# Loading the attention stages' weights and modulation tiles from GpSimd's queue instead of SyncE's

## The chip, the cores and the metric

The kernel runs on one core of a Trainium2 chip. A core has five engines, each with its own queue of instructions that it works off in order: TensorE (PE in the profile, with its weight loads shown apart as PEld), VectorE (DVE), ScalarE (ACT), GpSimd (POOL) and SyncE (SP). SP does no arithmetic; here it issues DMA transfers. Any of these queues can hold a DMA issue, and an issue that has to wait (for its target buffer to come free, say) holds up what stands behind it in the same queue. The transfers themselves run on 16 DMA engines that all queues share.

The metric is the time in microseconds (us) of one execution on the chip; less is better. Times of kernels are medians of several executions.

## The reference

A decoder trunk of two layers, for one sequence of 512 positions and 1024 features, in float32. A conditioning vector `c` gives, for each layer, six vectors of modulation (shift, scale and gate for each half of a layer). Cut to what matters here:

```
for layer in range(2):
    mod = silu(c) @ w_mod[layer] + b_mod[layer]        # 1024 x 6144, split into six vectors
    shift1, scale1, gate1, shift2, scale2, gate2 = split(mod, 6)
    h = rmsnorm(x, g_attn[layer]) * (1 + scale1) + shift1
    proj = h @ w_in[layer]                             # q, k, v of three groups of heads, and fz
    qa, ka, qb, kb = rotary(qa, ka, qb, kb)
    oa = differential_attention(qa, ka, va, lam)       # 4 heads (A)
    ob = dilated_mixture_attention(qb, kb, vb)         # 6 heads (B)
    oc = forgetting_attention(qc, kc, vc, cumsum(log_sigmoid(fz + bias)))   # 6 heads (C)
    x = x + gate1 * (concat(oa, ob, oc) @ w_out[layer])
    h = rmsnorm(x, g_mlp[layer]) * (1 + scale2) + shift2
    u, g = split(h @ w_up[layer])
    x = x + gate2 * ((silu(causal_conv3(g)) * u) @ w_down[layer])
return rmsnorm(x, g_final)
```

## The kernel before

**Layout and precision.** The activations are kept feature-major: `x` is a tile of 128 partitions, 8 chunks of features and 512 positions. Each operand of a big product is split into a high and a low part of float32r, and a product is three matmuls (`mm3`, L250 to L253): high by high, high by low, low by high. The weights are split on the chip: a raw weight tile of 128 x 1024 (512 KB) is loaded (`raww`), ACT copies its high part (L174, `whi`), and DVE subtracts to get its low part (L186, `wlo`).

**The weight pipeline.** `plan` lists all weight tiles of the program in the order of use. The class `Weights` walks along it: `dma` issues loads (L148) into a pool of 3 raw buffers, `hi` and `lo` make the two parts (a pool of 2 pairs), and `use` hands them to the matmuls. `pump`, called once per chunk of a product, keeps loads two tiles ahead and splits one tile ahead. A load waits until `wlo` of the tile three places earlier has been made, since that frees its buffer.

**The modulation.** `mod_stream` (L211 on) loads a row block of `w_mod` of 512 KB (L214, `rawm`) into a pool of 2 buffers, and DVE multiplies and sums it into a column of `modc` (L217). In the startup the first 16 blocks come in as `mu` (L1010) and are multiplied on POOL (L1036, then summed on ACT, L1037) or reduced on DVE; blocks 16 to 39 of layer 0 are streamed during layer 0's attention, the remaining 56 during layer 0's MLP.

**The attention of a layer** (`layer_attn`) works through eight pairs of heads in the order B0 B1 A0 C0 A1 C1 B2 C2. For each pair, 8 blocks of 128 queries go through scores, mask and maximum (DVE, L641), exponential (ACT), transposition, splitting and the product with the values; the loop runs over 64 blocks, with the second half of a block two blocks behind. Between these pieces `fill` puts the next pair's projections (`qkps`, L251 to L253) and values, and at the end the first parts of the output projection. `tick` advances small generators: `qk_post` copies a projection out of PSUM (`qf`, L456) and, for kinds A and B, needs its even and odd partitions exchanged for the rotation, which two DMA copies of 128 KB do (`sw`, L458 and L459); for kind A another 24 small copies stack the split rows (L477), for kind C `stack_gen` splits the rows (L420 on DVE, L434 on ACT) and copies in bias rows from `aT` (L443). `fz_post` runs the chain for the forget gate: a polynomial on DVE (`z`, up to L529), a cumulative sum on PE (`pf`, L537), its scaling on DVE (L541), the filling of a tile `au` with ones on POOL (L550) and the copying of values into it (L552, L553).

**What sets the order.** The Python code gives the order in which instructions are recorded; a scheduler of the framework then sets the order in each engine's queue by its own estimates, with some instructions told to come after others (`issue_after`). In the version before, all of the loads and copies named above are issued by SP (`nc.sync`), so `raww`, `rawm`, `sw`, `qk` and the bias rows stand in one queue; POOL has two small loads (`bm`, `gA`), the eight multiplications of `mu`, and the two fills of `au`.

Of the kernel before, what the change touches and what calls it, by code (L numbers as in the profile page):

```python
# [30 lines left out]
def kernel(  # L31
# [25 lines left out]
    nc = tc.nc  # L57
    PS = bass.MemoryType.PSUM
    V, A, T, G = nc.vector, nc.scalar, nc.tensor, nc.gpsimd
# [25 lines left out]
    def tick():  # L85
        for g in list(aux):
            if next(g, StopIteration) is StopIteration:
                aux.remove(g)
# [27 lines left out]
    for l in range(DEPTH):  # L116
# [16 lines left out]
        for m in range(KC):  # L133
            for b in range(0, FC, 8):
                n = min(8, FC - b)
                plan += [(wdown[l, m, :, 128 * b:128 * (b + n)], 128 * n, "wp" if m < 7 else "hs")]

    class Weights:
        def __init__(self):
            self.raw, self.w = {}, {}  # L140
            self.nd = self.nh = self.nl = self.nu = 0
            self.pt = None

        def dma(self, upto):
            while self.nd < min(upto, len(plan)):
                src, n, at = plan[self.nd]
                t = rawp.tile([128, 4 * VZ], F32, tag="raw", name="raww")
                nc.sync.dma_start(out=t[:, 0:n], in_=src)  # L148
                self.raw[self.nd] = t
                self.nd += 1  # L150

# [57 lines left out]
    W = Weights()  # L209

    def mod_stream(l, ci):  # L211
        part, m = divmod(ci, 8)
        raw = mrp.tile([128, 1024], F32, tag="raw", name="rawm")
        nc.sync.dma_start(out=raw, in_=wmod[l, ci])  # L214
        yield
        dst = modc[:, l, ci:ci + 1]
        V.tensor_tensor_reduce(out=raw, in0=raw, in1=scb, scale=1.0, scalar=bm[:, l, ci:ci + 1],  # L217
                               op0=ALU.mult, op1=ALU.add, accum_out=dst)
        yield
        yield  # L220
        yield
        if m < 7:
            return
        c = slice(8 * part, 8 * part + 8)
        if part in (1, 4):
            g = gA if part == 1 else gM
            V.scalar_tensor_tensor(out=scl[:, l, part // 4, :], in0=modc[:, l, c], scalar=1.0,
                                   in1=g[:, l, :], op0=ALU.add, op1=ALU.mult)
# [123 lines left out]
    def prep():  # L352
        lp = lpt[0]
        for l in range(DEPTH):
            lam_init = 0.8 - 0.6 * math.exp(-0.3 * l)
            V.tensor_scalar(out=sg[:, l:l + 1], in0=sg[:, l:l + 1], scalar1=1.0 - lam_init, scalar2=None, op0=ALU.mult)
            pr = sm.tile([128, 2, 32], F32, tag="lam", name="pr", bufs=1)
            V.tensor_tensor(out=pr, in0=lp[:, l, 0::2, :], in1=lp[:, l, 1::2, :], op=ALU.mult)
            sd = sm.tile([128, 2], F32, tag="lam2", name="sd", bufs=1)
            V.tensor_reduce(out=sd, in_=pr, axis=AX.X, op=ALU.add)  # L360
            with tc.issue_after(ss["pre"]):
                A.activation(out=sd, in_=sd, func=AF.Exp)
            V.scalar_tensor_tensor(out=nlam[:, l:l + 1], in0=sd[:, 1:2], scalar=-lam_init, in1=sd[:, 0:1],
                                   op0=ALU.add, op1=ALU.subtract)

    def layer_attn(l, ap, mods, st, rt0):
# [134 lines left out]
        def after(g):  # L501
            while True:
                with tc.issue_after(anchor[0]), tc.issue_after(anchor[1]):
                    if next(g, StopIteration) is StopIteration:
                        return
                yield
# [83 lines left out]
        def fill(idx, share):  # L590
            f = fills[idx]
            f[2] += share * f[1]
            n = 0
            while f[0] and f[2] > 0.3:
                if next(f[0][0], StopIteration) is StopIteration:
                    f[0].pop(0)
                    continue
                f[2] -= 1.3 if getattr(f[0][0], "__name__", "") == "v_half" else 0.65
                n += 1
                tick()  # L600
            if n == 0:
                tick()
# [29 lines left out]
        def emit_max(b):  # L632
            idx, kind, hh, i = blocks[b]
            n = 128 * (i + 1)
            scale = 32 ** -0.5 if kind == "A" else 0.125
            mask = C_BM if kind == "B" else C_CM
            res = []
            for s in S.pop(b):
                e = tmp("e", "e")
                nm = sm.tile([128, 1], F32, tag="nm", name="nm")  # L640
                anchor[0] = V.tensor_tensor_reduce(out=e[:, 0:n], in0=s[:, 0:n], in1=cst[:, mask + SEQ - n:mask + SEQ],  # L641
                                       scale=-scale, scalar=3e38, op0=ALU.add, op1=ALU.min, accum_out=nm).ins
                res.append((e, nm))
            E[b] = res

        def emit_exp(b):
            idx, kind, hh, i = blocks[b]
            n = 128 * (i + 1)
            if hh == 0 and i == 0:
                dens[idx] = sm.tile([128, 4, 2], F32, tag="dens", name="dens", bufs=3)  # L650
            res = []
            for mp, (e, nm) in enumerate(E[b]):
                den = sm.tile([128, 1], F32, tag="den", name="den") if mp else dens[idx][:, i, hh:hh + 1]
                anchor[1] = A.activation(out=e[:, 0:n], in_=e[:, 0:n], func=AF.Exp, bias=nm, scale=-1.0, accum_out=den).ins  # L654
                res.append((e, den))
            E[b] = res
# [16 lines left out]
        def emit_T(b):  # L673
            i = blocks[b][3]
            e = E.pop(b)
            if i == 1:
                pt = pts[b - 1][0]
            else:
                pt = ps_t.tile([128, SEQ], F32, tag="pt", name="pt")
            for j in range(i + 1):  # L680
                c = 128 * (i + j) if i < 2 else 128 * j
                T.transpose(pt[:, c:c + 128], e[:, 128 * j:128 * j + 128], ident)
            if i % 2 == 0:
                n = (384, 1024)[i // 2]
                pts["cur"] = tuple(ap.tile([128, n], F32R, tag="%s%d" % (t, i), name=t, bufs=1) for t in ("pth", "ptl"))
            pts[b] = (pt,) + pts["cur"]
# [11 lines left out]
        def emit_hi(b):  # L698
            if blocks[b][3]:
                p3, dh, dl = pt_views(b)  # L700
                A.activation(out=dh, in_=p3, func=AF.Copy)

        def emit_lo(b):
            if blocks[b][3]:
                p3, dh, dl = pt_views(b)
                V.tensor_tensor(out=dl, in0=p3, in1=dh.bitcast(F32), op=ALU.subtract)
# [87 lines left out]
        def ready(b):  # L794
            idx, kind, hh, i = blocks[b]
            if hh or i:
                return
            while (idx, 1) not in qks:
                fill(idx - 1, 0.1)
            while not done(idx):  # L800
                tick()

        emit_S(0)
        lag = 2
        f1, f2, f3 = 0.06, 0.055, 0.055
        for b in range(nb + lag):
            idx = blocks[min(b, nb - 1)][0]
            while idx and fills[idx - 1][0]:
                fill(idx - 1, 1.0)
            p = b - lag  # L810
            if l == 0 and b == 6:
                lpt.append(mrp.tile([128, 1024], F32, tag="raw", name="lp")[:, 0:256].rearrange(
                    "p (l j d) -> p l j d", l=DEPTH, j=4))
                nc.sync.dma_start(out=lpt[0], in_=lamp)
            if l == 0 and b == 10:
                with tc.issue_after(anchor[0]), tc.issue_after(anchor[1]):
                    prep()
            if b == 3:
                aux.append(after(fz_post()))
            if p >= 0:  # L820
                emit_T(p)
            if b < nb:
                emit_max(b)
            if p >= 0:
                emit_hi(p)
            fill(idx, f1)
            if b < nb:
                emit_exp(b)
            if p >= 0:
                emit_lo(p)  # L830
            fill(idx, f2)
            if b + 1 < nb:
                ready(b + 1)
                emit_S(b + 1)
            if b < nb:
                emit_norm(b)
            fill(idx, f3)
            if p >= 0:
                emit_PV(p)
            ms, mr = 4, 1.75  # L840
            if b >= ms:
                for _ in range(int((b - ms + 1) * mr) - int((b - ms) * mr)):
                    next(modg, None)
        aux.append(modg)
        for idx in range(8):
            while fills[idx][0]:
                fill(idx, 1.0)
        while any(g.__name__ == "head_post" for g in aux):
            tick()
        wl = W.use()  # L850
# [330 lines left out]
```

## Time and profile before

| | us |
|---|---|
| median of 3 runs | 1337.87 (1335.4 to 1338.98) |
| the profiled execution, its own time | 1334.63 |
| span in the profile, first to last instruction | 1332.9 |
| startup, layer 0's attention | 0 to 60, 60 to 290 |
| layer 0's MLP | 290 to 690 |
| layer 1's attention, layer 1's MLP | 690 to 925, 925 to 1333 |

The stages are cut by hand at round numbers near to where the lines of one stage end and those of the next begin. A row of the timeline gives the start, the busy time, the engine, the line, the operation, output and inputs with shapes, how many instructions are joined in the row, and in brackets the idle time of the engine just before and what ended it. A row of the waits gives who waited, for whom, how long in all, how many times, and the longest. "SPq" and "POOLq" mean the queue of an engine rather than its arithmetic. The granted clock of TensorE over the whole program is 0.989.

### The profile page before, as it was taken

The numbers are of one execution on the slowest core, as the hardware profiler recorded it, in microseconds if no ns is written. First come the engines' busy times: TensorE is split into PE (matmuls) and PEld (weight loads), VectorE is DVE, ScalarE is ACT, GpSimd is POOL, SyncE is SP. The second block draws the span as 40 slices with busy tenths as digits, with TensorE's granted clock in tenths as the row PEclk, the third lists the DMA queues.
The fourth block names the chain that finished last, engine by engine and source line by source line (L and its number), as shares of the span: only waits on it lengthen the run. The fifth ranks groups of instructions, "written<-read, shape, count | busy, mean of one in ns | idle before, by whom it ended". The sixth has DMA issues, their size and how long they took to land.

```text
span 1332.9 us, 17722 instructions
## 1 busy us (share of the span) xinstructions
PE 1277.8 (96%) x6568; PEld 1058.6 (79%) x6568; DVE 858.2 (64%) x1600; ACT 642.3 (48%) x1158; POOL 22.9 (2%) x16
## 2 busy tenths in 40 slices
PE   4899999999999999999999999999999999999997
PEld 1788888788877778888898888878878888888886
DVE  6888999868888874423347788875754444443232
ACT  5576677745333243322336677785543333333231
POOL 5100000000000000000000000000000000000000
PEclk8899999999999999999999999999999999999999
DMA  9345454433888853332432334212133333332331
GB/s 373 140 141 183 152 180 136 130 110 129 269 261 266 267 173 95 91 103 87 117 110 95 90 103 141 66 56 90 48 109 96 97 95 95 95 91 87 103 99 63
DMA packets 56601, 174.39 MB, mean 131 GB/s; under 512 B 8130, under 2 KB 10450, under 8 KB 56516
## 3 DMA queue, kind: packets, MB, share of 16 engines
q1 hardware_dynamic: 55364, 172.16, 41.0%
q8 instruction: 52, 0.85, 0.3%
q10 hardware_dynamic: 1088, 1.05, 0.2%
q14 instruction: 33, 0.27, 0.1%
q0 software_dynamic: 64, 0.06, 0.0%
HBM read 159.41 MB, written 2.10 MB: 121 GB/s over the span
## 4 chain that ended last, share of the span: by engine, by line
PE 53%; DMA 8%; DVE 7%; ACT 4%; issue 3%; SPq 0%; DVEq 0%; ACTq 0%
DMA rawm<-in_wmod_dram 7%; PE dps L251 6%; PE dps L253 6%; PE dps L252 6%; PE pu L251 4%; PE pu L253 4%; PE pu L252 4%; PE pg L252 4%; PE pg L253 4%; PE pg L251 4%; DVE wlo L186 1%; DVE rawm L217 1%; PE qkps L251 1%; PE qkps L252 1%; PE qkps L253 1%
## 5 line engine op out<-in xcount | busy, mean ns | idle before, releaser
L186 DVE TENSOR_TENSOR wlo<-raww,whi 128x1024 fp32r<-128x1024 f32 (+3 forms) x188 | 224.2, 1193 | 241.0 <-ACT whi L174 236.5
L174 ACT ACTIVATE whi<-raww 128x1024 fp32r<-128x1024 f32 (+3 forms) x188 | 194.5, 1035 | 329.6 <-PE dps L252 137.7
L253 PE MATMUL pu<-hh,wlo 128*128 128x512 f32 (+1 forms) x368 | 141.2, 384 | 3.5 <-DVE wlo L186 3.5
L252 PE MATMUL pg<-hl,whi 128*128 128x512 f32 (+1 forms) x368 | 143.0, 389 | 1.5 <-DVE hl L300 1.5
L251 PE MATMUL pg<-hh,whi 128*128 128x512 f32 (+1 forms) x368 | 141.6, 385 | 1.6 <-ACT whi L174 1.6
L251 PE MATMUL pu<-hh,whi 128*128 128x512 f32 (+1 forms) x368 | 142.4, 387 | 0.5 <-ACT whi L174 0.5
L253 PE MATMUL pg<-hh,wlo 128*128 128x512 f32 (+1 forms) x368 | 140.9, 383 | 1.1 <-DVE wlo L186 1.1
L252 PE MATMUL pu<-hl,whi 128*128 128x512 f32 (+1 forms) x368 | 140.7, 382 | 0.0
L251 PE MATMUL dps<-mh,whi 128*128 128x512 f32 x308 | 121.5, 395 | 0.0
L253 PE MATMUL dps<-mh,wlo 128*128 128x512 f32 x308 | 121.5, 394 | 0.0
L252 PE MATMUL dps<-ml,whi 128*128 128x512 f32 x308 | 121.2, 393 | 0.0
L217 DVE CUSTOM_DVE_ANT_0 rawm<-rawm,scb,bm 128x1024 f32<-128x1024 f32 x80 | 102.3, 1279 | 23.7 <-DMA rawm<-in_wmod_dram 23.4
L654 ACT ACTIVATE e<-e,nm 128x256 f32<-128x256 f32 (+3 forms) x160 | 89.0, 557 | 33.0 <-DVE nm L641 29.9
L251 PE MATMUL qkps<-hh,whi 128*128 128x512 f32 x224 | 95.1, 424 | 4.7 <-ACT qk L434 4.1
L898 ACT ACTIVATE y<-y 128x512 f32<-128x512 f32 x44 | 27.8, 632 | 142.6 <-DVE y L895 142.6
L252 PE MATMUL qkps<-hl,whi 128*128 128x512 f32 x224 | 89.7, 400 | 0.0
L253 PE MATMUL qkps<-hh,wlo 128*128 128x512 f32 x224 | 89.6, 400 | 0.0
L253 PEld LDWEIGHTS pu<-hh,wlo 128*128 128x128 f32 x368 | 69.1, 188 | 22.1 <-DVE wlo L186 6.9
L641 DVE CUSTOM_DVE_ANT_0 e<-s,cst 128x256 f32<-128x256 f32 (+3 forms) x160 | 76.4, 481 | 12.0 <-PE s L628 3.7
L252 PEld LDWEIGHTS pg<-hl,whi 128*128 128x128 f32 x368 | 69.0, 188 | 17.7 <-DVE hl L300 3.1
L253 PEld LDWEIGHTS pg<-hh,wlo 128*128 128x128 f32 x368 | 69.0, 188 | 16.7 <-DVE wlo L186 1.9
L251 PEld LDWEIGHTS pg<-hh,whi 128*128 128x128 f32 x368 | 69.1, 188 | 16.0 <-ACT whi L174 2.0
(176 smaller groups left out, 2663.2 us busy)
## 6 DMA issues: line engine op xcount, KB each, us to landing
raww<-in_wup_dram SPq DMA_DIRECT2D x88, 512.0 KB
rawm<-in_wmod_dram SPq DMA_DIRECT2D x80, 512.0 KB
raww<-in_wqk_dram SPq DMA_DIRECT2D x32, 512.0 KB
raww<-in_wdown_dram SPq DMA_DIRECT2D x32, 512.0 KB
mu<-in_wmod_dram SPq DMA_DIRECT2D x16, 512.0 KB
raww<-in_wout_dram SPq DMA_DIRECT2D x16, 448.0 KB
raww<-in_wv_dram SPq DMA_DIRECT2D x12, 512.0 KB
raww<-in_wdown_dram SPq DMA_DIRECT2D x16, 384.0 KB
```

Of the source, the lines that this page charges most:

```text
L174: A.activation(out=h[:, 0:m], in_=self.raw[i][:, c:c + m], func=AF.Copy)
L186: V.tensor_tensor(out=lo[:, 0:m], in0=raw[:, c:c + m], in1=h[:, 0:m].bitcast(F32), op=ALU.subtract)
L217: V.tensor_tensor_reduce(out=raw, in0=raw, in1=scb, scale=1.0, scalar=bm[:, l, ci:ci + 1], op0=ALU.mult, op1=ALU.add, accum_out=dst)
L251: T.matmul(ps[:, c], w[0], rhs[0][:, c], start=first, stop=False, skip_group_check=True)
L252: T.matmul(ps[:, c], w[0], rhs[1][:, c], start=False, stop=False, skip_group_check=True)
L253: T.matmul(ps[:, c], w[1], rhs[0][:, c], start=False, stop=last, skip_group_check=True)
L641: anchor[0] = V.tensor_tensor_reduce(out=e[:, 0:n], in0=s[:, 0:n], in1=cst[:, mask + SEQ - n:mask + SEQ], scale=-scale, scalar=3e38, op0=A ...
L654: anchor[1] = A.activation(out=e[:, 0:n], in_=e[:, 0:n], func=AF.Exp, bias=nm, scale=-1.0, accum_out=den).ins
L898: last_silu[0] = A.activation(out=y, in_=y, func=AF.Silu).ins
```

## The change

`Weights` gets an attribute `q`, the queue for its loads, which is SyncE at first. `mod_stream` uses the same attribute. `layer_attn` sets it to GpSimd just ahead of the loop over blocks and back to SyncE after the last fill of the attention has been recorded, ahead of the output projection's end.

```
 class Weights:
     def __init__(self):
...
         self.pt = None
+        self.q = nc.sync

     def dma(self, upto):
...
-            nc.sync.dma_start(out=t[:, 0:n], in_=src)
+            self.q.dma_start(out=t[:, 0:n], in_=src)

 def mod_stream(l, ci):
...
-    nc.sync.dma_start(out=raw, in_=wmod[l, ci])
+    W.q.dma_start(out=raw, in_=wmod[l, ci])

 def layer_attn(...):
...
     f1, f2, f3 = 0.06, 0.055, 0.055
+    W.q = G
     for b in range(nb + lag):
...
     for idx in range(8):
         while fills[idx][0]:
             fill(idx, 1.0)
+    W.q = nc.sync
     while any(g.__name__ == "head_post" for g in aux):
         tick()
```

Lines of the changed kernel are one higher than before from `dma` on, two higher behind the first of the new settings, three behind the second. In the whole program SP's queue goes from 308 to 230 rows and POOL's from 13 to 71 (a row joins equal neighbours). 74 loads go over: 24 `rawm` and 25 `raww` in layer 0, 25 `raww` in layer 1.

POOL's queue from its first DMA on, before. This is all that it holds, up to the end of the program:

```order
L989 DMA bm<-in_bmod_dram 128x96
L989 DMA gA<-in_gattn_dram 128x16
L1036 ISA
L1036 TENSOR_TENSOR mu<-mu,scb 128x1024 x8
L550 MEMSET au 128x192 x2
```

The same place of POOL's queue now, up to the first fill of `au`:

```order
L992 DMA bm<-in_bmod_dram 128x96
L992 DMA gA<-in_gattn_dram 128x16
L215 DMA rawm<-in_wmod_dram 128x1024
L1039 ISA
L1039 TENSOR_TENSOR mu<-mu,scb 128x1024 x8
L149 DMA raww<-in_wv_dram 128x1024
L149 DMA raww<-in_wqk_dram 128x1024 x2
L149 DMA raww<-in_wv_dram 128x1024
L149 DMA raww<-in_wqk_dram 128x1024
L215 DMA rawm<-in_wmod_dram 128x1024
L149 DMA raww<-in_wqk_dram 128x1024
L551 MEMSET au 128x192
```

The first modulation load now stands ahead of the multiplications of the startup, directly behind the two small loads, and the fill of `au` stands behind seven loads of the attention.

SP's queue in the first part of layer 0's attention, before (the loads of weights and modulation lie among the rotation copies `sw`; `lp` and `rope` are small tables):

```order
L148 DMA raww<-in_wqk_dram 128x1024 x2
L814 DMA lp<-in_lamp_dram 128x256
L458 DMA sw<-qf 64x512
L459 DMA sw<-qf 64x512
L148 DMA raww<-in_wv_dram 128x1024
L148 DMA raww<-in_wqk_dram 128x1024
L458 DMA sw<-qf 64x512
L459 DMA sw<-qf 64x512
L214 DMA rawm<-in_wmod_dram 128x1024
L321 DMA rope<-in_rope_dram 128x2x512
L214 DMA rawm<-in_wmod_dram 128x1024
```

The same part now; the two loads at its head are those recorded ahead of the block loop:

```order
L149 DMA raww<-in_wqk_dram 128x1024 x2
L816 DMA lp<-in_lamp_dram 128x256
L459 DMA sw<-qf 64x512
L460 DMA sw<-qf 64x512
L459 DMA sw<-qf 64x512
L460 DMA sw<-qf 64x512
L322 DMA rope<-in_rope_dram 128x2x512
```

The copies and tables now stand alone in SP's queue, in the order that they had.

The scheduler also sets the other engines' instructions in the attention a little differently. On DVE, at the end of the forget gate's polynomial in layer 0 (`z`, with `z_813` the scaled sum; `e,nm` are the masked scores and their maximum, `op` an output of the head before), before:

```order
L462 TENSOR_TENSOR qf<-qf,rope 128x512
L527 SCALAR_TENSOR_TENSOR z_632<-z_632,z_633 128x24
L464 TENSOR_TENSOR sw<-sw,rope 128x512
L529 SCALAR_TENSOR_TENSOR z_631<-z_632,z_631 128x24
L641 ISA e,nm<-s,cst 128x384
L641 ISA nm 128x1
L466 TENSOR_TENSOR qf<-qf,sw 128x512
L641 ISA e,nm<-s,cst 128x512
L641 ISA nm 128x1
L541 TENSOR_SCALAR z_813<-pf 128x24
L741 TENSOR_TENSOR op_818<-po,ot 64x512
```

The same place now:

```order
L465 TENSOR_TENSOR sw<-sw,rope 128x512
L525 SCALAR_TENSOR_TENSOR z_632<-z_632,z_634 128x24
L642 ISA e,nm<-s,cst 128x384
L642 ISA nm 128x1
L528 SCALAR_TENSOR_TENSOR z_632<-z_632,z_633 128x24
L467 TENSOR_TENSOR qf<-qf,sw 128x512
L530 SCALAR_TENSOR_TENSOR z_631<-z_632,z_631 128x24
L187 TENSOR_TENSOR wlo<-raww,whi 128x1024
L542 TENSOR_SCALAR z_813<-pf 128x24
L421 TENSOR_TENSOR qk<-qf,qk 64x512
L742 TENSOR_TENSOR op_818<-po,ot 64x512
```

The last step of the polynomial (L529, now L530) moved behind the scores of a block (128 x 384) and behind the sum of the rotation (L466, now L467), and a `wlo` moved up to stand between it and the scaling of `pf`.

More of the change, by code (lines that the diff above doesn't have):

```diff
@@ L142, in __init__ @@
             self.pt = None
+            self.q = nc.sync
         def dma(self, upto):
@@ L147, in dma @@
                 t = rawp.tile([128, 4 * VZ], F32, tag="raw", name="raww")
-                nc.sync.dma_start(out=t[:, 0:n], in_=src)
+                self.q.dma_start(out=t[:, 0:n], in_=src)
                 self.raw[self.nd] = t
@@ L213, in mod_stream @@
         raw = mrp.tile([128, 1024], F32, tag="raw", name="rawm")
-        nc.sync.dma_start(out=raw, in_=wmod[l, ci])
+        W.q.dma_start(out=raw, in_=wmod[l, ci])
         yield
@@ L805, in layer_attn @@
         f1, f2, f3 = 0.06, 0.055, 0.055
+        W.q = G
         for b in range(nb + lag):
@@ L847, in layer_attn @@
                 fill(idx, 1.0)
+        W.q = nc.sync
         while any(g.__name__ == "head_post" for g in aux):
```

## The prediction

> **What bounds the kernel now.** The first view is the head of the profile page: the span, and how much of it each engine is busy.
>
> ```profile
> span 1332.9 us, 17722 instructions
> PE 1277.8 (96%) x6568; PEld 1058.6 (79%) x6568; DVE 858.2 (64%) x1600; ACT 642.3 (48%) x1158; POOL 22.9 (2%) x16
> ```
>
> PE is busy 1277.8 of 1332.9 us, so in the whole program there are 55 us in which PE stands, and a change that touches no matmul can win only from these. POOL is nearly empty: 22.9 us in 16 instructions. Next comes the table by stages, cut where the kernel's stages meet: the startup, attention of layer 0, its MLP, attention of layer 1, its MLP. Columns are the busy times of PE, PEld, DVE, ACT and POOL, then the granted clock, the busy share of the DMA engines and GB/s.
>
> ```profile
> 0.00:60.00 60.00, 36.17 (x124) 23.31 (x125) 44.28 (x78) 29.27 (x46) 22.63 (x15) 0.83 0.64 248
> 60.00:290.00 230.00, 222.19 (x1322) 188.64 (x1321) 202.93 (x487) 164.27 (x360) 0.00 (x0) 0.99 0.50 156
> 690.00:925.00 235.00, 230.62 (x1430) 197.67 (x1430) 180.23 (x444) 165.72 (x366) 0.00 (x0) 1.00 0.30 92
> ```
>
> The two attention stages, where the loads change queue, leave PE idle for 7.8 us (230 − 222.19) and 4.4 us (235 − 230.62). In layer 0 DVE is busy 202.93 of 230 us, so it is nearly a second bound there; POOL does nothing in either. The startup has 24 us of PE idle. The third view is what ended PE's idle time: one row of layer 0's attention and one of layer 1's (total, times, longest).
>
> ```profile
> PE qkps L251 <- ACT qk L434: 4.1, 2, 2.1
> ```
> ```profile
> PE s L618 <- DVE nm L641: 0.9, 1, 0.9
> ```
>
> Neither names a DMA: PE waits for compute. What one step further back waits for a DMA is in the same view for DVE and ACT, here the rows with a DMA as the releaser, layer 0 and then layer 1:
>
> ```profile
> DVE qf L462 <- DMA sw<-qf: 0.5, 2, 0.3
> ACT wv L174 <- DMA raww<-in_wout_dram: 0.6, 1, 0.6
> ACT whi L174 <- DMA raww<-in_wqk_dram: 0.5, 1, 0.5
> ```
> ```profile
> DVE qf L462 <- DMA sw<-qf: 1.4, 2, 0.8
> ACT wv L174 <- DMA raww<-in_wout_dram: 0.5, 1, 0.5
> ACT wv L174 <- DMA raww<-in_woutl_dram: 0.4, 1, 0.4
> ```
>
> So rotation copies (`sw`) cost DVE 1.9 us in all, and weight loads cost ACT 2.0 us in four waits. On the other side stand SP's own waits, first layer 0, then layer 1:
>
> ```profile
> SPq L148 <- DVE wlo L186: 54.1, 16, 9.4
> SPq L214 <- DVE modc L217: 32.8, 9, 9.9
> ```
> ```profile
> SPq L148 <- DVE wlo L186: 82.5, 14, 14.1
> ```
>
> SP stands long behind a load that waits for its buffer (54.1 us, up to 9.4 at a time; 82.5 in layer 1), and copies queued behind it could be late. The rows above say they seldom are. One pair of copies shows why:
>
> ```profile
> 78.98 0.58 ACT L456 ACTIVATE qf<-qkps 128x512 f32<-128x512 f32 x1
> ...
> 79.65 0.33 SPq L148 DMA_DIRECT2D raww<-in_wqk_dram  x1
> ...
> 80.08 0.47 SPq L458 DMA_DIRECT2D sw<-qf  x1
> ```
>
> ACT finished `qf` at 79.56; a weight load went ahead of the copy at 79.65, and the copy left at 80.08, half a microsecond late. The order of SP's queue already fits the times at which buffers come free.
>
> **The change part by part.** It removes nothing: 74 loads (24 modulation and 25 weight tiles in layer 0, 25 weight tiles in layer 1) are issued by POOL instead of SP, waiting for the same buffers.
>
> *Copies.* They lose the loads ahead of them. The gain is at most the 0.5 + 1.4 = 1.9 us of DVE waits above, and none if landing, not issue, is what DVE waits for. PE has no row for it, so I take −0.5 (0 to −1.9).
>
> *Loads.* What POOL's issue costs is shown only by two small loads of the startup, the rows of the timeline (start, duration) and of the DMA view (KB, us to landing); a 512 KB load from SP is in the chain of waits:
>
> ```profile
> 1.25 0.70 POOL L989 DMA_DIRECT2D bm<-in_bmod_dram  x1 [0.80 <-POOLq L1170]
> 1.95 0.54 POOL L989 DMA_DIRECT2D gA<-in_gattn_dram  x1
> ```
> ```profile
> bm<-in_bmod_dram POOLq DMA_DIRECT2D x1, 48.0 KB, 4.1
> gA<-in_gattn_dram POOLq DMA_DIRECT2D x1, 8.0 KB, 4.8
> ```
> ```profile
> 336.79 4.72 DMA rawm<-in_wmod_dram
> ```
>
> An issue takes POOL 0.54 to 0.70 us, so 74 take about 46 us on an engine that is idle for all 230 + 235 us of these stages: 0. Landing is 4.1 to 4.8 us for small loads, against 4.72 us for a big one from SP. If POOL's own path adds time, it is paid where ACT already waits for a load, at four places: at worst a whole landing each, 4 × 4.8 = 19 us; at best the four waits go, −2.0. I take 0, since loads are mostly issued a full tile ahead. A load that SP held behind another wait also goes earlier.
>
> The Trainium skill ("DMA: Bandwidth & Descriptors", "Specifications") speaks against the change: first byte after about 1 µs from GpSimd's path, 0.6 µs from SyncE's. An estimate from that page would be 4 × 0.4 = 1.6 us more, a sum of +2.4 in place of +0.8; no run here shows the two side by side.
>
> *Startup.* The scheduler places the first modulation load of layer 0 directly behind `gA` in POOL's queue, where it waits for nothing. Before, SP issued it at 58.98. It now falls into the stretch where every byte counts:
>
> ```profile
> 10.00:20.00 10.00, 5.35 (x7) 2.35 (x8) 5.67 (x9) 7.42 (x12) 2.17 (x2) 1.00 1.02 410
> ```
> ```profile
> 7.90 14.41 SPq L1010 DMA_DIRECT2D mu<-in_wmod_dram  x12
> ```
> ```profile
> 58.98 0.42 SPq L214 DMA_DIRECT2D rawm<-in_wmod_dram  x1
> ```
> ```profile
> 9.31 2.33 POOL L1036 TENSOR_TENSOR mu<-mu,scb 128x1024 f32<-128x1024 f32 x1 [6.83 <-DMA mu<-in_wmod_dram]
> ...
> 11.68 1.06 ACT L1037 ACTIVATE mu<-mu 128x1024 f32<-128x1024 f32 x1 [3.18 <-POOL mu L1036]
> ```
>
> From 10 to 20 us the DMA engines are full (share 1.02, 410 GB/s), and `mu` loads go out one per 14.41/12 = 1.2 us. Another 512 KB (524,288 bytes) at 410 GB/s is 1.28 us. POOL's first multiplication (9.31) and ACT's reduction (11.68) wait for such a load, and all of the startup's chain hangs on them, so I take the whole **+1.28** (0 if the scheduler's early load slips into a gap). What is won at 58.98 is nothing, as no row waits for that tile.
>
> *The au fill.* `MEMSET au` stands in POOL's queue, now behind a weight load that waits for DVE's `wlo`:
>
> ```profile
> 38.07 0.25 POOL L550 MEMSET au<- 128x192 f32 x1
> ...
> 90.86 0.18 DVE L552 COPY au<-z 128x24 f32<-128x24 f32 x1
> ```
>
> Before, it ran at 38.07, 53 us ahead of its reader. Now an issue of 0.70 and the fill of 0.25 may come between `wlo` and the copy: 0 to +1, and behind that copy DVE's whole queue would stand. I take 0, because DVE has more work between the two.
>
> *Order.* Around 85 to 95 us DVE's order changes: two instructions now run ahead of `z` L529, on which PE's `pf` waits, and a `wlo` moves up into an idle place.
>
> ```profile
> 86.38 0.55 DVE L641 CUSTOM_DVE_ANT_0 e<-s,cst 128x384 f32<-128x384 f32 x1
> ...
> 86.85 0.69 DVE L466 TENSOR_TENSOR qf<-qf,sw 128x512 f32<-128x512 f32 x1
> ...
> 89.01 0.18 DVE L541 TENSOR_SCALAR z<-pf 128x24 f32<-128x24 f32 x1 [0.86 <-PE pf L537]
> ```
>
> That is 0.55 + 0.69 = 1.24 us later for `pf`, while DVE's idle 0.86 is filled. Over all, the new order could undo the two gaps behind L434 (−4.1) or open as much elsewhere (+4.1); the rows just shown cancel nearly, so 0.
>
> **Sum:** +1.28 − 0.5 + 0 = **+0.8 us**. The profiled execution took 1334.63 us (span 1332.9 and 1.7 around it), so it would become 1335.4. The median of the runs, 1337.87 (1335.4 to 1338.98), is 3.2 above that execution; the forecast for a median is **1338.7**.
>
> **The rivals.** *Faster: copies and order both pay.* The startup still costs 1.3, but DVE's 1.9, ACT's 2.0 and PE's 4.1 all go: 1337.87 + 1.3 − 1.9 − 2.0 − 4.1 = 1331.2. For it speaks that SP stood 54.1 and 82.5 us behind buffers; against it, that PE's waits name no DMA.
>
> *Slower: POOL's loads land late.* Where ACT waits for a load, half of a landing is added: 4 × 2.4 = 9.6, so 1348.3. It decides wherever a tile's buffer comes free less than a landing ahead of ACT's copy. Against it: 4.8 us of landing for 8 KB from POOL is no worse than 4.72 for 512 KB from SP.
>
> *Slower: POOL's issues and DVE block each other.* The trace shows DVE suffering from POOL's work in the startup:
>
> ```profile
> 18.89 4.51 DVE L186 TENSOR_TENSOR wv<-raww,wv 128x1024 fp32r<-128x1024 f32 x2 [0.26 <-ACT wv L174]
> ```
> ```profile
> L186 DVE TENSOR_TENSOR wlo<-raww,whi 128x1024 fp32r<-128x1024 f32 (+3 forms) x188 | 224.2, 1193 | 241.0 <-ACT whi L174 236.5
> ```
>
> Beside POOL's multiplications this subtraction takes 4.51/2 = 2.26 us, against a mean of 1.19. If issuing blocked DVE too, layer 0's 49 issues × 0.62 = 30 us would fall on a DVE with 230 − 202.93 = 27 us of slack, layer 1's 25 × 0.62 = 15.5 on one with 235 − 180.23 = 55. At half of the sum where DVE is busy, (0.88 × 30 + 0.77 × 15.5)/2 = 19 us: 1357. Against it: an issue is not a multiplication that reads two tiles.
>
> The Trainium skill ("SBUF — State Buffer", "Who interferes with whom") says that DVE with two SBUF inputs contends with a GpSimd instruction that reads SBUF, not with one that only writes it. The slow subtraction agrees; by that rule writing descriptors leaves it alone, and this rival would be 0.
>
> *Nothing changes:* all loads wait for the same buffers, and even the startup hides its 1.28: 1337.9. It lies inside the forecast.
>
> **How the numbers follow.** A measurement of this kernel tells about 0.3%, 4.0 us, from no change. The forecast, with "nothing changes", has 0.52 (own range 1334 to 1342); faster 0.20 (1331.2); late loads 0.20 (1348.3); blocking 0.08 (1357). The range takes in all but the last and the tails: 1331 to 1349. Faster is 0.20, same 0.52, slower 0.20 + 0.08 = 0.28.
>
> **What would show it.** Startup: POOL's first multiplication later than 9.31 and PE's start by about 1.3. Copies: DVE's waits for `sw` below 0.5 and 1.4. Loads: ACT's waits for `raww` still under 1 us; tens of them would mean late loads. Blocking: L186's mean well above 1193 ns inside attention. Order: the two L434 gaps of 2.1 us still there. If PE's busy time in 60 to 290 falls or rises by over 4 us against its stretch, the order did more than I allow, and the forecast is wrong.

## The result, and the profile after

The changed kernel takes 1356.11 us (median of 4 runs, 1353.79 to 1358.78) against 1337.98 of the kernel before in the same set: **18.1 us slower, ratio 1.0139** (95% interval 1.0115 to 1.0163). The forecast was 1338.7 in a range of 1331 to 1349. The time lies above the range.

The head of the page of the changed kernel:

```profile
span 1354.0 us, 17796 instructions
PE 1286.2 (95%) x6568; PEld 1062.3 (78%) x6568; DVE 859.1 (63%) x1600; ACT 642.5 (47%) x1158; POOL 62.4 (5%) x90
```

The arithmetic has hardly changed: DVE 859.1 us (858.2 before), ACT 642.5 (642.3). POOL went from 22.9 to 62.4; the rise is its 74 issues of loads, at 0.53 us each. So the 21.1 us that the span grew are not more work for these engines. Where they arise is read from PE's rows in the timeline: the first scores of layer 0 (`s`), the first matmul of its MLP (`pg`), the first projection of layer 1 (`qkps`), and the first of its MLP. Before:

```profile
64.62 0.22 PE L618 MATMUL s<-qk 128*128 128x128 f32 x1
...
307.21 0.28 PE L251 MATMUL pg<-hh,whi 128*128 128x256 f32 x1
...
689.74 0.39 PE L251 MATMUL qkps<-hh,wv 128*128 128x256 f32 x1 [0.34 <-ACT wv L174]
...
951.14 0.28 PE L251 MATMUL pg<-hh,whi 128*128 128x256 f32 x1
```

The same four instructions in the changed kernel:

```profile
66.27 0.30 PE L619 MATMUL s<-qk 128*128 128x128 f32 x1
...
324.90 0.28 PE L252 MATMUL pg<-hh,whi 128*128 128x256 f32 x1
...
708.01 0.39 PE L252 MATMUL qkps<-hh,wv 128*128 128x256 f32 x1 [0.27 <-ACT wv L175]
...
971.69 0.28 PE L252 MATMUL pg<-hh,whi 128*128 128x256 f32 x1
```

The lags are 1.65, 17.69, 18.27 and 20.55 us. So the startup cost 1.65, **layer 0's attention 16.04**, its MLP 0.6, layer 1's attention 2.3, the rest 0.55. What DVE and PE waited for in layer 0's attention (60 to 300 us) is in the view of waits, DVE's two rows first:

```profile
DVE qf L463 <- DMA sw<-qf: 13.0, 5, 3.6
...
DVE qf L463 <- DMA qk<-qf: 3.6, 1, 3.6
```
```profile
PE po L730 <- DVE ptl L707: 5.7, 5, 1.6
PE qkps L252 <- ACT qk L435: 3.5, 2, 2.1
PE po L729 <- ACT e L655: 2.3, 1, 2.3
```
```profile
SPq L459 <- ACT qf L457: 89.5, 6, 24.7
```

DVE's waits at the first step of the rotation, which overwrites `qf` and so has to wait for the copies that read it, rose from 0.5 to 16.6 us, and PE stands behind what DVE then delivers late (`ptl`, or `e` by way of ACT). What the 16.04 us are made of shows in the stretch from the first scores to the first matmul of the MLP, before and then after (columns as in the prediction's table by stages; before, POOL does nothing in it):

```profile
64.62:307.21 242.59, 234.67 (x1405) 200.05 (x1405) 209.59 (x495) 167.58 (x367) 0.00 (x0) 0.99 0.47 145
```
```profile
66.27:324.90 258.63, 240.24 (x1403) 203.58 (x1404) 209.66 (x495) 167.99 (x367) 24.98 (x48) 0.97 0.45 135
```

PE's idle time rose from 7.92 to 18.39 us, by 10.5; its busy time rose by 5.6 with not a matmul more, at a granted clock of 0.97 instead of 0.99. Whether the stalls bring the lower clock was not tested.

SP's row shows that the change did what it says: until the last copies of the stage, no wait of SP is at a load, and the rotation copies wait mostly for their data (`qf`). They leave at once, and yet they arrive later. The first rotation of the block loop shows how. Before, the load of `wv` is issued behind the two copies, on the same queue:

```profile
72.13 0.47 SPq L458 DMA_DIRECT2D sw<-qf  x1
72.66 0.59 SPq L459 DMA_DIRECT2D sw<-qf  x1
73.34 1.25 SPq L148 DMA_DIRECT2D raww<-in_wv_dram  x1
...
75.85 0.69 DVE L462 TENSOR_TENSOR qf<-qf,rope 128x512 f32<-128x512 f32 x1
```

In the changed kernel POOL issues the same load while SP issues the second copy:

```profile
73.87 0.47 SPq L459 DMA_DIRECT2D sw<-qf  x1
74.39 0.60 SPq L460 DMA_DIRECT2D sw<-qf  x1
74.42 0.53 POOL L149 DMA_DIRECT2D raww<-in_wv_dram  x1 [5.38 <-DVE wlo L187]
...
79.33 0.69 DVE L463 TENSOR_TENSOR qf<-qf,rope 128x512 f32<-128x512 f32 x1 [1.82 <-DMA sw<-qf]
```

From the first copy's issue to DVE's start it is 3.72 us before and 5.46 now, of which DVE stood idle for 1.82. Over the eight rotations of this stage, DVE starts a median of 2.45 us after the second issue has ended before (1.46 to 3.80), and 4.37 us now (3.75 to 5.58).

### The profile page after: what moved, and what is told of

It reads as the page before. It is cut to its first block, busy times and chain, and to the rows that moved or that the text cites. A ratio compares the mean times of both kernels' runs of the same rounds, so it can differ in the third digit from the quotient of the medians.

```text
span 1354.0 us, 17796 instructions
## 1 busy us (share of the span) xinstructions
PE 1286.2 (95%) x6568; PEld 1062.3 (78%) x6568; DVE 859.1 (63%) x1600; ACT 642.5 (47%) x1158; POOL 62.4 (5%) x90
## 4 chain that ended last, share of the span: by engine, by line
PE 50%; issue 8%; DMA 8%; DVE 6%; ACT 2%; POOL 0%; DVEq 0%; SPq 0%; ACTq 0%; POOLq 0%
DMA rawm<-in_wmod_dram 6%; PE dps L252 5%; PE dps L253 5%; PE dps L254 5%; PE pu L252 4%; PE pu L254 4%; PE pu L253 4%; PE pg L253 4%; PE pg L254 4%; PE pg L252 4%; DVE rawm L218 1%; PE qkps L252 1%; DVE wlo L187 1%; PE qkps L253 1%; PE qkps L254 1%
## 5 line engine op out<-in xcount | busy, mean ns | idle before, releaser
L218 DVE CUSTOM_DVE_ANT_0 rawm<-rawm,scb,bm 128x1024 f32<-128x1024 f32 x80 | 102.4, 1281 | 22.9 <-DMA rawm<-in_wmod_dram 22.1
```

## The experiments

The theory formed from these rows (**C**): copies and loads share the DMA engines. In one queue, a load that is issued behind a copy does not delay it; in another queue, it does, and the copy's lateness stands in front of DVE, which this stage is nearly bound by. (What it says of the other queue is too simple; this is taken up behind the run with only the rotation copies on POOL.) Its rivals: the new **order** on DVE, ACT and PE (O), and POOL's **way of issuing** (P). The scheduler sets the order on PE, DVE and ACT anew in most of these runs. It is the changed kernel's to the row in the run with two loads of half a row and in the one for the startup, and all but a few instructions of DVE and ACT in the two runs with fewer bytes on POOL. In the others the total holds the new order's share too, and the waits say more.

**The loads made small.** The change kept, with an eighth of each load's bytes on POOL, so that the weights and modulations computed are not the reference's:

```
-                self.q.dma_start(out=t[:, 0:n], in_=src)
+                if self.small:
+                    self.q.dma_start(out=t[:, 0:128], in_=src[:, 0:128])
+                else:
+                    self.q.dma_start(out=t[:, 0:n], in_=src)
...
+            return t[:, 0:128].unsqueeze(1).to_broadcast([128, m // 128, 128])
...
+            W.q.dma_start(out=raw[:, 0:128], in_=wmod[l, ci][:, 0:128])
...
-        W.q = G
+        W.q, W.small = G, True
```

> The changed kernel with the same instructions in the same order on all five engines, but each load that POOL issues brings only 128 of its 1024 columns (64 KB instead of 512); the high and low parts are made from these columns read eight times, and the modulation sum reads scb twice, so that the weights and modulations of these tiles are not the reference's. Theory C (the rotation and stacking copies share the DMA engines with POOL's loads, land 2 us and more later, and DVE waits for them): DVE's waits at L463 in layer 0's attention go from 16.6 us to under 2, layer 0's attention loses 12 us or more, and the total is 1338 to 1342. Theory O (the other order of DVE, ACT and PE costs the time) and theory P (POOL's issue or the slow start of its transfers costs it): the total stays at 1350 to 1356.

It took 1337.5 us, ratio 1.0004 (0.9995 to 1.0014), a little under theory C's 1338 to 1342. DVE's waits in the same stretch, and the landing of the copies in the view of DMA issues (KB, median us from issue to landing). The trace dates only 3 of the 16 landings, here and in the changed kernel:

```profile
DVE qf L483 <- DMA qk<-qf: 1.1, 1, 1.1
...
DVE qf L483 <- DMA sw<-qf: 0.7, 2, 0.4
```
```profile
sw<-qf SPq DMA_DIRECT2D x16, 128.0 KB, 2.2
```

The same view of the changed kernel:

```profile
sw<-qf SPq DMA_DIRECT2D x16, 128.0 KB, 4.3
```

With nearly the same order, the same queues and as many issues, the copies land after 2.2 us instead of 4.3, DVE waits 1.8 us for them instead of 16.6, and the whole loss is gone. That rules out order and issuing as causes of any size: what costs is the loads' bytes on the way.

**The control.** The kernel before with the same cut of bytes, all on SP (the edit is the same, without the change of queue).

> The kernel before with the same cut of bytes at the same tiles (64 KB instead of 512, these weights and modulations not the reference's), all loads on SP. Theory C: in the kernel before the loads hardly cost anything, so it gains 0 to 4 us, 1334 to 1338; what then remains between this run and the one of the changed kernel with small loads is the new order's share, and C wants it under 4 us. Theory O: that difference stays at 12 us or more.

1336.32 us, ratio 1.0002 (0.9990 to 1.0014). In the kernel before, the bytes of these loads cost nothing that can be measured: by the interval, at most 1.3 us could be won from them. The medians of the two runs with small loads differ by 1.2 us, about what the startup loses in the one and not in the other, but the two intervals overlap.

**One queue again, POOL's.** All copies of the block loops are put among the loads:

```
-            nc.sync.dma_start(out=sw[0::2, :], in_=qf[1::2, :])
-            nc.sync.dma_start(out=sw[1::2, :], in_=qf[0::2, :])
+            W.q.dma_start(out=sw[0::2, :], in_=qf[1::2, :])
+            W.q.dma_start(out=sw[1::2, :], in_=qf[0::2, :])
...
-                        nc.sync.dma_start(out=res[m][32 * j:32 * j + 32, :].bitcast(F32), in_=...)
+                        W.q.dma_start(out=res[m][32 * j:32 * j + 32, :].bitcast(F32), in_=...)
```

> The changed kernel with the rotation, stacking and bias copies of the block loop on POOL's queue too, so that loads and copies stand in one queue again. Theory C in the form that a queue works off its transfers in order, so that a copy never shares with loads issued behind it: DVE's waits at the rotation fall below 5 us in layer 0, total 1336 to 1345. Theory P (POOL's way of issuing is what is slow): copies land still later, DVE waits for more than 16 us in layer 0, total 1360 or more. Theory O: the order differs in part from the changed kernel's, total around 1350 to 1356.

1336.78 us, ratio 1.0006 (0.9994 to 1.0017). The first rotation in its timeline:

```profile
74.64 0.53 POOL L459 DMA_DIRECT2D sw<-qf  x1 [5.36 <-ACT qf L457]
75.16 0.54 POOL L460 DMA_DIRECT2D sw<-qf  x1
75.70 0.54 POOL L149 DMA_DIRECT2D raww<-in_wv_dram  x1
...
77.79 0.69 DVE L463 TENSOR_TENSOR qf<-qf,rope 128x512 f32<-128x512 f32 x1
```

The load stands right behind the copies, and DVE starts 3.15 us after the first issue without an idle moment. The loads themselves stay on POOL in this run, so their own way through POOL's queue is not what costs. POOL's queue serves as well as SP's, if the copies share it with the loads.

**The mirror.** The kernel before, loads on SP, with the rotation copies on POOL (`G.dma_start` at L458 and L459).

> The mirror of the change: the kernel before, all loads on SP, the rotation copies on POOL. Theory C-any: the copies land late, 4 us or more after the second issue, DVE waits 6 us or more for them in layer 0, total 1343 to 1356. Theory C-pool (POOL's transfers crowd out those of SP): the copies are now on the favoured side, DVE's waits stay under 2 us and the total is 1333 to 1340.

1356.2 us, ratio 1.0145 (1.0130 to 1.0160): as slow as the change, and just over the end of C-any's 1343 to 1356. Here even the first copies, ahead of the block loop, lose their cover. In the kernel before SP issues them at 53.15 to 56.74 and four loads from 57.38 on, and DVE starts at 58.15. In the mirror (SP, POOL, DVE):

```profile
53.80 0.33 SPq L148 DMA_DIRECT2D raww<-in_wv_dram  x1
54.18 0.42 SPq L214 DMA_DIRECT2D rawm<-in_wmod_dram  x1
```
```profile
53.64 0.57 POOL L458 DMA_DIRECT2D sw<-qf  x1 [15.54 <-ACT qf L456]
54.21 0.54 POOL L459 DMA_DIRECT2D sw<-qf  x1
```
```profile
61.19 0.69 DVE L462 TENSOR_TENSOR qf<-qf,rope 128x512 f32<-128x512 f32 x1 [7.42 <-DMA rawm<-in_wmod_dram]
```

The loads go out beside the copies, and DVE starts at 61.19, 3.0 us later than before. From there to the end of the stage DVE waits 8.1 us for copies. So neither side is favoured: loads on SP crowd out copies on POOL too. That the totals are equal is partly chance, for the loss lies elsewhere: by PE's rows, 3.8 us ahead of the first scores, 12.6 in layer 0's attention and 6.5 in layer 1's, where the change lost 1.65, 16.0 and 2.3.

**Copies on ACT** (`nc.scalar.dma_start` at L458 and L459, loads on SP):

> The kernel before, all loads on SP, but the rotation copies (L458, L459) issued from ACT's queue. Theory C-any (copies that stand in another queue than the loads share the engines with loads issued later, whichever queues these are): DVE starts on the copies 4 us or more after the second issue (2.5 before), DVE's waits for them in layer 0 are 6 us or more instead of 0.5, total 1343 to 1352. Theory C-pool (only POOL's transfers crowd out others): landing as before, under 3 us, and the total is 1335 to 1341, where up to 4 us would be ACT's own time for 36 issues of some 0.5 us.

1346.25 us, ratio 1.0075 (1.0050 to 1.0100), with these waits in layer 0's attention:

```profile
DVE qf L462 <- DMA sw<-qf: 6.2, 4, 2.4
```

So POOL is not needed for the loss. That ACT also pays some 0.5 us for each of its 40 issues is not taken apart here, so of the 10 us only DVE's part is seen to be C's.

**Only weights, or only modulation, on POOL** (the one `dma_start` of the two is `nc.sync` again).

> The changed kernel with only the weight tiles on POOL; the modulation tiles stay on SP, with the copies. By theory C each load on another queue than the copies counts: layer 0 has 25 of its 49 left there, so about half of its 16 us is lost, layer 1's 2.9 stay, the startup's 1.4 go (no early modulation tile): 8 + 3 = 11 above before, 1348. If the two kinds of load don't count alike: weight tiles alone near 1340 or near 1355.

> The changed kernel with only the modulation tiles on POOL; the weight tiles stay on SP, with the copies. Theory C: 24 of 49 loads, about half of layer 0's 16 us, plus the startup's 1.4, nothing in layer 1: 1346. If the two kinds don't add up (the sum of this run's and the weight tiles' run's loss differs from the changed kernel's 18 by more than 5), the collisions depend on which load meets a copy and not on how many there are.

1346.04 us (ratio 1.0078, 1.0053 to 1.0103) and 1345.77 us (1.0066, 1.0049 to 1.0082). The two losses add up to 1.44%, against 1.39% of the change, as C wants it.

**Half the bytes, and half the rows.** Half of each tile loaded and read twice (256 KB); and, apart from it, all of each tile as two loads of 512 columns. The changed kernel ran beside them as their measure.

> As the run with small loads (same order on all engines, weights and modulations not the reference's), but half of each tile is loaded (256 KB) and read twice. Theory C with bytes as its measure: the 12 to 16 us of layer 0 shrink to about half, total 1343 to 1349. If rows count and not bytes alone (2 KB rows, and half as many bytes), nearly all is gone: 1337 to 1342.

> The changed kernel, the same order on PE, DVE, ACT and SP, but each load of POOL is issued as two loads of 512 columns, so that its rows are 2 KB as those of the copies, not 4 KB. If the DMA engines take turns between the queues row by row, the copies get half of an engine instead of a third: DVE's start after the second issue goes from a median of 4.4 to about 3.3 us, and layer 0's loss of 16 us to about 9; total 1346 to 1350. If what counts is the bytes in flight: no change, 1353 to 1358. If POOL's issues count (twice as many): slower than 1358.

> The changed kernel once more, on the chip of the other runs of this set, as their measure: ratio 1.0139 again, within 0.3% (1.011 to 1.017).

The changed kernel came to 1356.06 us against 1335.51 before (ratio 1.0157, 1.0140 to 1.0174); half the bytes to 1345.79 (1.0082, 1.0067 to 1.0097); two loads of half a row each to 1353.79 (1.0142, 1.0127 to 1.0157). So 512 and 256 KB a load lose 20.6 and 10.3 us, and 64 KB, measured in another set, about 0.5: the loss goes with the bytes. With rows of 2 KB instead of 4 KB the interval overlaps that of the change, and DVE starts a median of 3.94 us after the second issue, against 4.01 in the changed kernel beside it and 3.3 forecast. So the forecast of 1346 to 1350 by turns of a row each is wrong.

**Only the rotation copies among POOL's loads** (L459, L460 to `W.q`; stacking and bias copies stay on SP).

> The changed kernel with the rotation copies (L459, L460) on POOL's queue, among the loads, while stacking and bias copies stay alone on SP. If the rotation copies' lateness is all of layer 0's loss: the startup's 1.4 stay, total 1337 to 1341. If the stacking copies (24 for each q and each k of kind A), which still stand in another queue than the loads, carry a part of it: layer 0 loses 4 to 8 us at the two A pairs (around 115 to 130 and 165 to 185 us), total 1342 to 1348.

1341.89 us, ratio 1.0045 (1.0029 to 1.0061): between the two forecasts. Most of the loss is the rotation copies'. Of what is left, one piece is not the stacking but a load ahead in the same queue (POOL, then DVE):

```profile
110.78 0.53 POOL L149 DMA_DIRECT2D raww<-in_wqk_dram  x1 [3.99 <-DVE wlo L187]
111.42 0.53 POOL L459 DMA_DIRECT2D sw<-qf  x1
```
```profile
117.81 0.69 DVE L463 TENSOR_TENSOR qf<-qf,rope 128x512 f32<-128x512 f32 x1 [3.80 <-DMA sw<-qf]
```

The copies were issued right behind a 512 KB load, and DVE waited 3.80 us, out of 4.5 for copies in the block loop of layer 0. So standing in the loads' queue doesn't help a copy whose load is ahead of it. How much of the rest the stacking copies carry stays open.

Is it then the queue that counts, or the moment of issue? Landings that the traces date one by one speak for the moment. In layer 1 of the mirror, one load on SP goes out between the issues of two copies on POOL (SP's row, POOL's rows, then the view of DMA issues for the first copy and for the second):

```profile
765.71 0.33 SPq L148 DMA_DIRECT2D raww<-in_wv_dram  x1
```
```profile
765.20 0.55 POOL L458 DMA_DIRECT2D sw<-qf  x1 [20.27 <-ACT qf L456]
765.74 0.55 POOL L459 DMA_DIRECT2D sw<-qf  x1
```
```profile
sw<-qf POOLq DMA_DIRECT2D x1, 128.0 KB, 2.0
```
```profile
sw<-qf POOLq DMA_DIRECT2D x1, 128.0 KB, 4.2
```

The first copy, 0.51 us ahead of the load, landed after 2.0 us; the second, 0.03 behind it, after 4.2. The changed kernel has a copy at 874.35 with POOL's load 0.47 us behind it, and it landed after 2.1. With all in POOL's queue, a copy at 82.38, 0.53 us behind a load, landed after 4.0. So a load just ahead of a copy, or together with it, delays the copy in either arrangement, and a load half a microsecond behind it hardly does (at most, the mirror shows 3.2 us with such a load). What the shared queue gives is the spacing: a load recorded behind a copy is issued about half a microsecond after it or later. No run moved the moment alone and kept the queues.

**The startup.** The first modulation tile back on SP, the order on PE, DVE and ACT unchanged:

```
-        W.q.dma_start(out=raw, in_=wmod[l, ci])
+        (nc.sync if ci == 16 else W.q).dma_start(out=raw, in_=wmod[l, ci])
```

> The changed kernel, but the first modulation tile of layer 0 is issued by SP again (the order on PE, DVE and ACT is that of the changed kernel, to the row). Theory S (the startup's 1.4 us come from this tile's 512 KB among the mu loads): POOL's first multiplication goes from 10.67 back to 9.3, PE's drift at 60 us is about 0 instead of 1.4, and the total is 1.4 us below the changed kernel, 1354.7. Rival (the startup was delayed by POOL being busy with the issue, or by chance): no change of the total beyond 0.5 us either way, or PE's drift at 60 us stays above 1.

1352.41 us against 1336.89, ratio 1.0115 (1.0097 to 1.0132). POOL's first multiplication in this run, and in the changed kernel:

```profile
9.23 2.34 POOL L1039 TENSOR_TENSOR mu<-mu,scb 128x1024 f32<-128x1024 f32 x1 [6.76 <-DMA mu<-in_wmod_dram]
```
```profile
10.67 2.33 POOL L1039 TENSOR_TENSOR mu<-mu,scb 128x1024 f32<-128x1024 f32 x1 [7.68 <-DMA mu<-in_wmod_dram]
```

The start is back where it was (9.31 before), and so are the first scores (64.56, against 64.62 before and 66.27 in the changed kernel), so the early load is the cause. But its bytes are not the measure. The same row in the run with 64 KB, and in the one with 256 KB:

```profile
10.68 2.33 POOL L1059 TENSOR_TENSOR mu<-mu,scb 128x1024 f32<-128x1024 f32 x1 [7.68 <-DMA mu<-in_wmod_dram]
```
```profile
10.11 2.34 POOL L1059 TENSOR_TENSOR mu<-mu,scb 128x1024 f32<-128x1024 f32 x1 [7.11 <-DMA mu<-in_wmod_dram]
```

An eighth of the bytes delays the start as long as the whole (10.68), half of them by 0.8. The total is lower than the changed kernel's by more than 1.4 us, but the two were measured in different sets whose intervals overlap.

## Why the prediction was wrong

**The step that failed is *Copies*.** It said: "They lose the loads ahead of them. The gain is at most the 0.5 + 1.4 = 1.9 us of DVE waits above", and took −0.5, with 0 as the worst. In place of it, layer 0's attention lost 16 us, with DVE's waits for copies up by 16.1. The step looked only at what stands ahead of a copy in the queue. That a queue also holds back the loads behind a copy, and that this kept their bytes out of its way, wasn't weighed: the sum had no term for transfers that meet. The rows for it were there. The prediction used the DMA engines being full to price the startup, and it quoted this stage's DMA share of 0.50; by an estimate from its landing of 4.72 us, 49 loads take 231 us, so that in 230 us a load is on its way nearly all the time. With DVE busy for 202.93 of 230 us, two more microseconds on each of eight rotations had nowhere to hide. The waits and the lag agree well in this execution (16.1 and 16.04), but that is partly chance: 5.6 us of the lag are busy time of PE, and in the second execution profiled, DVE waited 14.9 us for copies in the block loop and layer 0 lost 12.5.

The Trainium skill ("DMA: Bandwidth & Descriptors", "Issuing engines are not separate DMA queues") says that transfers of all issuing engines run on the same 16 DMA engines and interleave. The landing of 4.3 us against 2.2 agrees; the prediction took no price from it.

**Startup: right in size, not in its working.** +1.28 was forecast as 512 KB at 410 GB/s; POOL's first multiplication moved from 9.31 to 10.67, by 1.36, and the run with that one load back on SP undid it. But 64 KB cost the same, so the quotient of bytes and bandwidth is not what the delay is made of; what it is made of stays open.

**Loads: right.** Their own lateness was put at 0. ACT's waits for `raww` in layer 0's attention are now:

```profile
ACT whi L175 <- DMA raww<-in_wqk_dram: 1.3, 1, 1.3
...
ACT wv L175 <- DMA raww<-in_wout_dram: 0.6, 1, 0.6
```

That is 1.9 us, against 1.1 before. It is over the 1 us that the prediction named as its sign, but far from the tens that would have meant late loads; the rival in which loads land late (1348.3) falls by it.

**The au fill: right.** POOL filled it at 92.8, and its reader came at 95.9, with no wait before it.

```profile
L553 DVE COPY au<-z x2: 174/174/175, 95.9 to 96.1; 128x24 f32<-128x24 f32 x2
...
L551 POOL MEMSET au<- x1: 278/278/278, 92.8 to 92.8; 128x192 f32 x1
```

**Order: right at 0.** The two gaps behind L434 are still there (3.5 us in two), and the run with small loads, in the changed kernel's order, is as fast as the kernel before. The prediction's last sign would have blamed the order all the same: PE's busy time from 60 to 290 us, read at these fixed times, fell by 10.5 us, from 222.19 to 211.69. That sign could not tell a new order from late copies.

**The blocking rival had the right time (1357) for the wrong reason.** Its mark was a longer `wlo`. In 60 to 300 us, before and then after:

```profile
L186 DVE TENSOR_TENSOR wlo<-raww,whi 128x1024 fp32r<-128x1024 f32 x21 | 25.6, 1218 | 1.4 <-ACT whi L174 1.1
```
```profile
L187 DVE TENSOR_TENSOR wlo<-raww,whi 128x1024 fp32r<-128x1024 f32 x20 | 24.4, 1219 | 1.0 <-ACT whi L175 0.9
```

1218 and 1219 ns: POOL's issuing does not slow this subtraction. The rule of the Trainium skill weighed there ("SBUF — State Buffer", "Who interferes with whom") holds here.

**Not settled:** layer 1's 2.3 us, where 25 loads in 235 us meet copies less often, were not taken apart; nor was the mirror's 6.5 us there, nor what the early load does to the startup, nor whether the queue matters beyond the moment of issue, nor how the DMA engines divide themselves between two queues, beyond that the bytes count and the length of the rows hardly does.

## What to carry to other kernels

A queue that carries both big loads and small urgent copies is also an order of transfers: a load recorded behind a copy is issued after it and hardly delays it here, while one ahead of it does. Before loads are moved to a queue of their own "out of the way", look for what waits for the small transfers, and count how often a load would be in flight beside them; SP's long waits at a load's buffer cost nothing that could be measured here. To test such a suspicion, shrink the bytes and leave every instruction in its place.

## What was not expected of the hardware

Two transfers of 128 KB between partitions land after 2.2 us with loads of 64 KB from another queue beside them, and after 4.3 with loads of 512 KB (three dated landings each). In one queue, with a load issued 0.54 us behind the second, a pair landed after 2.7 and 2.5, and DVE didn't notice. Both directions cost: loads on POOL and copies on SP 1.0139, the reverse 1.0145, though not in the same places.
